# Four warm-up matmuls, two of them fp32, in place of twelve bf16 ones, in a weight-gradient kernel

## The chip, the cores and the metric

The kernel runs on one core of a Trainium2 chip. A core has a matrix engine (TensorE, "PE" in the profile, with its weight loads shown apart as "PEld"), VectorE (DVE), ScalarE (ACT), GpSimd (POOL) and SyncE (SP), each with its own instruction stream, and 16 DMA engines that they share. Engines wait for each other by semaphores. The metric is the time of one execution on the device in microseconds (us), lower is better.

## The reference

The gradient of a weight matrix: two fp32 inputs are multiplied and summed over the batch and over the rows of each batch element.

```python
batch, m, k, n = 16, 512, 1024, 768
input        # (16, 512, 1024) float32
grad_output  # (16, 512, 768)  float32
grad_weight = np.einsum('bmk,bmn->kn', input, grad_output)   # (1024, 768) float32
```

Batch and rows together make one contraction of 8192; the output has 1024 x 768 elements.

## The kernel before

The 8192 rows are cut into 64 slices of 128, since the matrix engine contracts over 128 partitions. A slice of `input` is 128 x 1024 and one of `grad_output` 128 x 768. Both output dimensions are halved (K into two halves of 512, each of four tiles of 128 columns; N into two halves of 384), so a slice needs 16 matmuls with a 128 x 128 stationary tile and a 128 x 384 moving tile, all in bf16 with fp32 sums in PSUM.

The 64 slices come in 32 loads of two. Nine loads are plain ("s" in `LOADS`): each of their slices is used in four products A, B, C and D, one for each quarter of the output. The other 23 ("P") are combined in pairs: VectorE adds and subtracts the halves of two slices, and seven products (A, D, m, n, o, p, q) do the work of eight. Their partial sums are kept in `acc` and `macc` in SBUF and carried into and out of eight PSUM banks by VectorE and ScalarE copies. Which product runs next, over how many loads, is written out by hand in the string `ORDER`; each of the four compute engines takes its instructions in program order.

The loads on the GpSimd queue convert fp32 to bf16 on the way (L113, L114, L118 and L120). The first slices are an exception, so that work can begin early: `gf` (slice 0 of `grad_output`, in two halves on SP's queue, L88 and L90) and `xf` (slices 0 and 1 of `input`, on ScalarE's queue, L89 and L91) arrive as fp32, and VectorE and ScalarE round them to bf16 piece by piece in `round_by` (L211). The first real matmuls (L337) wait for these roundings. Slice 1 of `input` is rounded just before the step that needs it.

At the very beginning stands the part that the change touches. With the four DMAs of the first slices issued, the matrix engine multiplies constant ones by constant ones twelve times (L96) into the PSUM bank `bank7`, and nothing ever reads the result. The operands are the constant tiles of the framework, written by four GpSimd memsets before the engines are let go: one column of ones, read again and again. A bf16 matmul is two instructions in the program, one that loads the stationary tile and one that streams the moving tile. The warm-up waits for nothing and, being first in the matrix engine's program, all real matmuls stand behind it.

Of the kernel before, what the change touches and what calls it, by code (L numbers as in the profile page):

```python
# [9 lines left out]
P = 128  # L10
# [25 lines left out]
    "l20 l21 l22 t20 t21 t22 t10 t11 t12 t13 l23 t23 l10 l11 l12 l13 l30 l31 l32 l33 "  # L36
).split()

WARMUP = [512] * 10 + [128] * 2
PAIRS_HELD = 14  # L40
SUMS_HELD = 9

# [4 lines left out]
def kernel(  # L47
# [6 lines left out]
    nc = tc.nc  # L54
    bf16 = mybir.dt.bfloat16
    f32 = mybir.dt.float32
# [33 lines left out]
    nc.sync.dma_start(out=gf[:, RIGHT], in_=G[0:P, RIGHT])  # L90
    nc.scalar.dma_start(out=xf[1], in_=X[P : 2 * P, :])  # L91

    ones = nc.const_aps.tensor(1.0, (P, P), bf16)
    wps = psum.tile([P, 512], f32, name="bank7")
    for cols in WARMUP:
        nc.tensor.matmul(  # L96
            wps[:, 0:cols],
            ones,
            nc.const_aps.tensor(1.0, (P, cols), bf16),
            start=True,  # L100
            stop=True,
        )
# [349 lines left out]
```

## Time and profile before

| What | Value |
|---|---|
| Time, median of 4 runs (lowest to highest) | 163.27 us (163.19 to 163.5) |
| The profiled execution's own time | 163.33 us |
| Its span, from the first to the last instruction | 161.6 us |
| PE busy | 156.6 us, 97% of the span, 950 matmuls |
| DVE / ACT / POOL busy | 140.8 / 117.9 / 34.6 us |
| Warm-up matmuls (L96) | 12 |
| Real matmuls (L337 and L392) | 938 |

The profile is one execution of the program. Times in it count from the start of the span; 1.73 us of the execution's own time lie outside it. In a timeline a row merges instructions of a kind: its start, its length, its engine and line, what it writes and reads with the shapes, how many there are, and in square brackets how long the engine had been idle before and what ended that. A matmul's end is modelled and overlaps the next one's start, so the rate of the matrix engine is read from the distance between starts, not from a matmul's length.

### The profile page before, as it was taken

How to read it: one execution, taken by the hardware profiler on the slowest of the kernel's cores; microseconds unless marked ns; L12 is line 12 of the kernel's file. 1: busy time of each engine (PE TensorE's matmuls, PEld its weight loads, DVE VectorE, ACT ScalarE, POOL GpSimd, SP SyncE). 2: the span in 40 equal slices, each digit the busy share in tenths (PEclk: the TensorE clock that was granted, in tenths of full speed). 3: DMA queues.
4: the chain of work that ended last, by engine and by line, in shares of the span. 5: the costliest groups of instructions: out<-in, count | busy, mean ns of one | idle time of the engine just before them, and what ended most of it. 6: DMA issues, size and time to landing. Idle time of an engine off the chain costs nothing.

```text
span 161.6 us, 2781 instructions
## 1 busy us (share of the span) xinstructions
PE 156.6 (97%) x950; PEld 92.7 (57%) x950; DVE 140.8 (87%) x267; ACT 117.9 (73%) x278; POOL 34.6 (21%) x69
## 2 busy tenths in 40 slices
PE   8899999999999999999999999999999999999991
PEld 2465655655556665566655566656556665556561
DVE  0545878879889999999999999999997999999982
ACT  3745348446498899978999797997795666987730
POOL 7442222212222212222222222222122100000000
PEclk9999999999999999999999999999999999999999
DMA  5999999999999999999999999999999999900695
GB/s 180 294 213 211 215 212 212 215 214 213 214 211 211 213 212 213 213 213 213 214 213 214 212 215 212 214 211 214 215 211 216 208 215 211 197 5 0 228 355 198
DMA packets 12398, 33.40 MB, mean 207 GB/s; under 512 B 1376, under 2 KB 4192, under 8 KB 12384
## 3 DMA queue, kind: packets, MB, share of 16 engines
q0 software_dynamic: 9360, 28.64, 89.6%
q1 hardware_dynamic: 2592, 3.47, 6.1%
q10 hardware_dynamic: 432, 1.11, 1.8%
q8 instruction: 7, 0.11, 0.3%
q14 instruction: 7, 0.06, 0.1%
HBM read 58.72 MB, written 3.15 MB: 383 GB/s over the span
## 4 chain that ended last, share of the span: by engine, by line
PE 84%; DMA 13%; issue 1%; DVE 0%; POOLq 0%
PE bank L337 84%; DMA xp<-in_input_dram 9%; DMA gp<-in_grad_output_dram 4%; PE bank L392 0%; DVE acc L400 0%; POOLq L436 0%
## 5 line engine op out<-in xcount | busy, mean ns | idle before, releaser
L337 PEld LDWEIGHTS <-xp 128*128 128x128 bf16 x650 | 63.3, 98 | 44.2 <-DVE xp L211 1.3
L337 PE MATMUL bank<-gp,xp 128*128 128x384 bf16 x468 | 80.8, 327 | 0.9 <-DVE xp L211 0.7
L353 ACT COPY macc<-bank 128x384 f32<-128x384 f32 x91 | 39.3, 492 | 9.8 <-PE bank L337 9.4
L357 DVE TENSOR_TENSOR acc<-bank,acc 128x384 f32<-128x384 f32 x80 | 39.8, 551 | 6.1 <-PE bank L337 5.9
L337 PEld LDWEIGHTS <-xe 128*128 128x128 bf16 x276 | 26.9, 98 | 18.0 <-DVE xe L148 0.2
L353 ACT COPY acc<-bank 128x384 f32<-128x384 f32 x57 | 24.7, 484 | 13.8 <-PE bank L337 13.8
L296 ACT COPY bank<-macc 128x384 f32<-128x384 f32 x73 | 33.0, 493 | 1.6 <-DVE acc L357 0.9
L337 PE MATMUL bank<-ge,xp 128*128 128x384 bf16 x182 | 33.6, 326 | 0.0
L337 PE MATMUL bank<-gp,xe 128*128 128x384 bf16 x184 | 32.4, 327 | 0.0
L296 ACT COPY bank<-acc 128x384 f32<-128x384 f32 x47 | 21.5, 492 | 9.1 <-DVE acc L357 7.4
L114 POOL DMA_DIRECT2D xp<-in_input_dram x30 | 15.9, 530 | 52.9 <-DMA xp<-in_input_dram 28.5
L113 POOL DMA_DIRECT2D gp<-in_grad_output_dram x30 | 15.9, 532 | 37.5 <-PE bank L337 13.9
L357 DVE TENSOR_TENSOR macc<-bank,macc 128x384 f32<-128x384 f32 x35 | 18.0, 551 | 2.0 <-PE bank L337 2.0
L138 DVE TENSOR_TENSOR ge<-gp 128x1152 bf16<-128x1152 bf16 x23 | 17.3, 751 | 0.1
L148 DVE TENSOR_TENSOR xe<-xp 128x1024 bf16<-128x1024 bf16 x23 | 15.8, 685 | 0.8 <-DMA xp<-in_input_dram 0.7
L194 DVE TENSOR_TENSOR acc<-acc,macc 128x768 f32<-128x768 f32 (+1 forms) x20 | 16.1, 874 | 0.0
L337 PE MATMUL bank<-ge,xe 128*128 128x384 bf16 x92 | 15.9, 327 | 0.0
L157 DVE TENSOR_TENSOR xp<-xp 128x1024 bf16<-128x1024 bf16 x23 | 15.8, 685 | 0.0
L143 DVE TENSOR_TENSOR gp<-gp 128x768 bf16<-128x768 bf16 x23 | 12.8, 554 | 0.5
L152 DVE TENSOR_TENSOR xe<-xp 128x512 bf16<-128x512 bf16 x23 | 9.6, 418 | 0.0
L355 DVE COPY acc<-bank 128x384 f32<-128x384 f32 x6 | 3.2, 555 | 3.1 <-PE bank L337 3.0
L96 PE MATMUL bank<-const-bfloat16-1.0 128*128 128x512 bf16 (+1 forms) x12 | 4.0, 510 | 0.8 <-PEq L436 0.8
(18 smaller groups left out, 15.6 us busy)
## 6 DMA issues: line engine op xcount, KB each, us to landing
xp<-in_input_dram POOLq DMA_DIRECT2D x30, 512.0 KB, 16.8
gp<-in_grad_output_dram POOLq DMA_DIRECT2D x30, 384.0 KB, 16.8
out_dram<-acc SPq DMA_DIRECT2D x15, 192.0 KB, 2.4
xf<-in_input_dram ACTq DMA_DIRECT2D x2, 512.0 KB, 4.9
gp<-in_grad_output_dram POOLq DMA_DIRECT2D x3, 192.0 KB, 6.4
xp<-in_input_dram POOLq DMA_DIRECT2D x2, 256.0 KB, 7.7
gf<-in_grad_output_dram SPq DMA_DIRECT2D x2, 192.0 KB, 4.2
out_dram<-acc SPq DMA_DIRECT2D x1, 128.0 KB, 1.8
```

The source lines that it names most:

```text
L113: nc.gpsimd.dma_start(out=gp, in_=G[rows, :].rearrange("(p m) n -> p m n", m=2))
L114: nc.gpsimd.dma_start(out=xp, in_=X[rows, :].rearrange("(p m) k -> p m k", m=2))
L138: nc.vector.tensor_add(out=ge.rearrange("p a n -> p (a n)"), in0=g[:, 0 : 3 * NH], in1=g[:, NH : 4 * NH])
L143: nc.vector.tensor_sub(out=g[:, 0::3, :], in0=g[:, 0::3, :], in1=g[:, 2:0:-1, :])
L148: nc.vector.tensor_add(out=xe[:, 0:2, :].rearrange("p a k -> p (a k)"), in0=xp[:, 0, :], in1=xp[:, 1, :])
L152: nc.vector.tensor_add(out=extra[i][0][:, 2, :], in0=xp[:, 0, 0:KH], in1=xp[:, 1, KH:K])
L157: nc.vector.tensor_sub(out=x[:, 1:3, :], in0=x[:, 1:3, :], in1=x[:, 0::3, :])
L194: op(out=dst, in0=dst, in1=src)
L296: nc.scalar.copy(out=bank, in_=sum_of(p, q))
L337: nc.tensor.matmul(bank, stat, mov, start=opening and j == 0 and not carried, stop=close and j == len(items_now) - 1, skip_group_check=car ...
L353: nc.scalar.copy(out=dst, in_=bank)
L357: nc.vector.tensor_add(out=dst, in0=bank, in1=dst)
```

## The change

The list `WARMUP` no longer gives twelve widths but four pairs of a type and a width, and the loop takes both operands of a matmul, stationary and moving, from the constant ones of that type. The first and the last matmul stay as they were (bf16, 512 columns); the two in the middle are fp32, 512 columns. The other eight, six of 512 columns and two of 128, are gone. An fp32 matmul is one instruction in the program, which brings its own stationary tile with it.

```diff
-WARMUP = [512] * 10 + [128] * 2
+WARMUP = [("b", 512), ("f", 512), ("f", 512), ("b", 512)]
...
-    ones = nc.const_aps.tensor(1.0, (P, P), bf16)
+
     wps = psum.tile([P, 512], f32, name="bank7")
-    for cols in WARMUP:
+    for dt, cols in WARMUP:
+        dtype = f32 if dt == "f" else bf16
         nc.tensor.matmul(
             wps[:, 0:cols],
-            ones,
-            nc.const_aps.tensor(1.0, (P, cols), bf16),
+            nc.const_aps.tensor(1.0, (P, P), dtype),
+            nc.const_aps.tensor(1.0, (P, cols), dtype),
             start=True,
             stop=True,
         )
```

The programs of the other four engines and the real part of the matrix engine's program, its waits among them, are the same instruction by instruction. The two memsets of the constants that are now read stand in both kernels.

## The prediction

> **What bounds the kernel now.** I read the chain that ended last first, because it says which part of the span can move the end at all.
>
> ```profile
> 11 pieces in order of time: start us, us, what
> ...
> 1.23 6.15 DMA gp<-in_grad_output_dram
> 7.38 0.28 issue
> 7.66 14.14 DMA xp<-in_input_dram
> 21.80 0.04 issue
> 21.84 135.47 PE bank L337 x830
> ```
>
> Up to 21.84 us the end hangs on the input transfers, and from there on the matrix engine runs without a gap: 135.47 us / 830 = 0.163 us per matmul of 384 columns. A delay of the matrix engine before 21.84 therefore reaches the end only as far as it exceeds what the engine waits there anyway. Those waits are few; the timeline of the start has all three.
>
> ```profile
> 0.78 4.01 PE L96 MATMUL bank<-const-bfloat16-1.0 128*128 128x512 bf16 x12 [0.78 <-PEq L436]
> 5.17 2.15 PE L337 MATMUL bank<-gp,xp 128*128 128x384 bf16 x12 [0.39 <-DVE xp L211]
> 7.05 0.49 DVE L211 CAST xp<-xf 128x256 bf16<-128x256 f32 x2 [0.68 <-DMA xf<-in_input_dram]
> 7.60 6.68 PE L337 MATMUL bank<-gp,xp 128*128 128x384 bf16 x40 [0.28 <-DVE xp L211]
> 21.84 0.34 PE L337 MATMUL bank<-gp,xp 128*128 128x384 bf16 x1 [0.28 <-DMA xp<-in_input_dram]
> ```
>
> The reader is to see: warm-up from 0.78 to 4.79; a first block of 12 real matmuls at 5.17, released by a rounding; a second block at 7.60, released by the rounding of a transfer that landed at 7.05; and one more wait, for a transfer, at 21.84. The idle times count from a matmul's modelled end, which lies 0.327 - 0.163 = 0.16 us after the next one could start (0.327 is the length of one). So the second and third wait are really 0.28 + 0.16 = 0.44 us each. These are two cushions: the first block may be 0.44 us late for nothing, and what is left over meets another 0.44 at 21.84.
>
> The speed of the array at the start is read from the weight loads, one in front of each warm-up matmul:
>
> ```profile
> 2.44 0.15 PEld L96 LDWEIGHTS <-const-bfloat16-1.0 128*128 128x128 bf16 x1 [0.27 <-issue]
> 2.86 0.15 PEld L96 LDWEIGHTS <-const-bfloat16-1.0 128*128 128x128 bf16 x1 [0.28 <-issue]
> 3.29 0.15 PEld L96 LDWEIGHTS <-const-bfloat16-1.0 128*128 128x128 bf16 x1 [0.27 <-issue]
> 3.72 0.15 PEld L96 LDWEIGHTS <-const-bfloat16-1.0 128*128 128x128 bf16 x1 [0.28 <-issue]
> 4.07 0.54 PEld L96 LDWEIGHTS <-const-bfloat16-1.0 128*128 128x128 bf16 x3 [0.20 <-issue]
> ```
>
> The distance is 0.427 us for 512 columns, then 0.35, and the next matmul starts (4.06 and 4.28 in narrower windows) are 0.22 apart. So the rate doubles inside the matmul that starts at 3.71: with x us at the slow rate, x/0.427 + (0.35 - x)/0.213 = 1, x = 0.27, the change lies at 3.98. That is 3.20 us after the first matmul. The row PEclk shows full clock from the first slice on, so it doesn't show this halving. The first real block is already fast (12 matmuls in 2.15 us).
>
> **What the Trainium skill says.** "TensorE: Matmul & The Clock Gate", Part 1: the array starts at half clock and is released by about 3.4 us of sustained activity, watched in windows of 3.41 us. The trace agrees: 3.20 us. The same page, Part 4: transposes don't count as busy in the same way, so not every use of the array does; the trace has none, and no fp32 either. Its section on weight-path modes: fp32 has no fast weight load. "FP8 and Floating Point Precision", TensorE Precision Notes: a true fp32 product is four passes through the array.
>
> **The change, part by part.**
>
> Removed: eight bf16 matmuls and ten weight loads of bf16 (twelve before, two after). They are before 4.79 us and nothing reads their result. The program is 18 instructions shorter; I cost that at nothing, since warm-up matmuls were paced by the array, not by issue. Without that cover it would still end in the wait for 5.17.
>
> Added: two fp32 matmuls. The trace has no row for one. Four passes of 512 columns at the slow rate are 4 x 0.427 = 1.71 us each. The warm-up is then 2 x 0.427 + 2 x 1.71 = 4.27 us at the slow rate against 10 x 0.427 + 2 x 0.107 = 4.48 before. If the rate never changes within it, it ends at 0.78 + 4.27 = 5.05, before the data at 5.17. Upper bound: every pass has its own weight load that isn't hidden, at the 0.15 us of the rows above: 8 x 0.15 = 1.2 more, end at 6.27. Lower bound: two passes each, end at 3.34. I take four passes with the loads hidden for the length, so the length alone costs nothing.
>
> Moved: the moment at which the rate doubles. This is the item with a price, and it can't be read from the trace. Bounds: from below 3.98 as before (no gain: with the data at 5.17 there is nothing to win by an earlier release), from above two windows later, 3.98 + 2 x 3.41 = 10.80. What I choose: the fp32 stream does not release the clock. In the trace the release came from a stream without a gap; an fp32 matmul brings four sets of weights in one instruction, and nothing shows that these loads slip under the passes as the bf16 ones do (PE starts 0.427 apart, loads inside). With 0.58 us per pass the array streams for 0.427/0.58 = 74% of the time. Then the real matmuls must do it: released 3.20 us after 5.17, at 8.37.
>
> The sum for that: from 5.17 to 8.37 the real matmuls run at the slow rate, 0.427 x 384/512 = 0.320 us each, so 10 of the 12 are done, and the last two take 0.163 each: the first block ends at 8.70 in place of 7.16 (7.32 less the 0.16). Its data are there (VectorE's last rounding for the first block ends at 6.37, slice 1's first pieces are rounded by 7.6). The second block starts at 8.70, not 7.60: 1.10 us late, the first cushion spent. It has the transfers that it had, and at 21.84 it finds the second cushion: 1.10 - 0.44 = 0.66 us late from there to the end, since no later wait takes anything back. Profiled execution: 161.6 + 0.66 = 162.26 of span, with 1.73 outside it 163.99; it stands 0.06 above the median of the runs, so 163.93, taken as 163.9.
>
> What is queued behind: all real matmuls, and the copies out of PSUM that wait for them; VectorE and ScalarE idle in this stretch for PE in any case. POOL's loads up to 22 us wait for transfers only, so the transfers keep their times. No wait is added, no queue is passed.
>
> **The rivals.**
>
> Covered after all (same). fp32 passes count like bf16 ones. Release at 3.98; 3.20 us of the 4.27 are done by then, the rest takes 1.07/2 = 0.53, the end is at 4.51, before 5.17. Time: 163.3. For it: warm-up had 0.39 us to spare, and the cushions make it deaf: a release at T costs (T - 5.17)/2 of the first block, so up to T = 5.17 + 2 x 0.88 = 6.93 nothing is lost, and up to 7.6 less than can be measured. Against it: a release that fails in one window comes later than that. This one ends on the other side; it decides if the release falls before 7.6.
>
> Late release, or a long warm-up (slower still). If release only comes at window ends, at 10.80: (10.80 - 5.17)/0.320 = 17.6 matmuls are done by then, which the kernel before reaches at 7.60 + 5.6 x 0.163 = 8.51; late by 2.29, less 0.44 is 1.85: 165.1. Or the loads are exposed and the clock is not released: the real block starts at 6.27, released at 9.47, ends at 9.80, late by 2.20, less 0.44 is 1.76: 165.0. For it: the windows are not tied to the first real matmul. Against it: cold real matmuls stream without a gap and should fill the next window that they can.
>
> A faster one. The two cushions are bound by transfers that landed at 7.05 and 21.80. If these landed earlier, because the program fetch of PE is shorter and leaves the DMA engines alone, up to 0.44 us at 21.84 could be won: 162.8. Against it: the instruction queues hold 7 packets each and 0.3% and 0.1% of the engines' time, and 18 instructions fewer of some 1,900 move that by nothing.
>
> **How the numbers follow.** No release by fp32, 0.36: 163.9, its own range 163.5 to 164.6. Covered, 0.33: 163.3. Late or long, 0.24: 165.1, up to 166. Faster, 0.07. About 0.2% (0.33 us) is what a measurement of this kernel can tell from no change. So slower 0.60, same 0.33, faster 0.07. The range 163.0 to 165.6 leaves out most of the faster case and the upper part of the late one, some 0.14.
>
> **What would show it.** In the timeline after: the fp32 rows at L97, their length (1.71 us each at the slow rate), and the end of warm-up. Right: the first real matmuls start 0.32 apart, the rate doubles near 8.4, the second block starts near 8.7, the wait for a transfer near 21.84 is gone. Covered: the first twelve start 0.163 apart and 7.60 and 21.84 stand. Wrong altogether: an end that moves while 21.84 stands, or real matmuls that begin after 6.3.

## The result, and the profile after

The changed kernel takes 163.11 us (median of 43 executions, 162.89 to 163.57) against 163.30 us (62 executions, 163.05 to 163.75): ratio 0.9988, 95% interval 0.9983 to 0.9992. That is 0.19 us faster. It is less than the 0.2% that the forecast called measurable, but the interval excludes no change. The forecast was 163.9 and slower. The clock did not cost what the forecast charged for it, and the kernel gained in a place that the forecast had only as its least likely case.

The timeline of the start of the changed kernel (start, length, engine, line, what), which answers to the one shown of before:

```profile
0.77 0.59 PE L97 MATMUL bank<-const-bfloat16-1.0 128*128 128x512 bf16 x1 [0.77 <-PEq L437]
...
1.15 3.62 PE L97 MATMUL bank<-const-float32-1.0 128*128 128x512 f32 x4
...
2.00 0.34 PEld L97 LDWEIGHTS bank<-const-float32-1.0 128*128 128x128 f32 x1 [0.52 <-issue]
...
2.86 0.34 PEld L97 LDWEIGHTS bank<-const-float32-1.0 128*128 128x128 f32 x1 [0.52 <-issue]
...
3.71 0.15 PEld L97 LDWEIGHTS <-const-bfloat16-1.0 128*128 128x128 bf16 x1 [0.52 <-issue]
...
4.56 0.64 PE L97 MATMUL bank<-const-bfloat16-1.0 128*128 128x512 bf16 x1
...
5.18 9.01 PE L338 MATMUL bank<-gp,xp 128*128 128x384 bf16 x51
...
7.12 0.49 DVE L212 CAST xp<-xf 128x256 bf16<-128x256 f32 x2 [0.58 <-DMA xf<-in_input_dram]
```

The two fp32 matmuls appear as four rows, with one weight load each and 0.85 us from start to start (1.15 to 4.56 is four times 0.853). That is two passes of 0.427 us per row, so four per matmul, as the forecast took it, and the 0.34 us loads are hidden under the passes. In this execution the warm-up never left the half clock: the trace's record of the full clock begins at 5.87 us (3.98 in the profile before), which is called the release below. The real matmuls begin at 5.18 all the same. The first two start 0.29 and 0.32 us before the next, the rest about 0.16 apart, and the second block starts at 7.68, right behind its rounding.

The chain that ended last, of the changed kernel:

```profile
23 pieces in order of time: start us, us, what
...
30.09 17.15 DMA xp<-in_input_dram
...
47.86 17.50 DMA xp<-in_input_dram
65.36 0.05 issue
65.41 91.93 PE bank L338 x564
```

In the profile before, the chain left the transfers at 21.84 us. Here nothing waits at 21.84; in this execution the matrix engine instead waits at 65.41 (0.39 us from start to start beyond the usual 0.16) for a later transfer. So the two profiles have the same span, 161.6 us, though the medians differ; this one execution took 163.41 us by its own time, 0.30 above its median. One profile on each side could not settle it. The forecast had listed the missing wait at 21.84 as a sign of its own case, the late release; as the experiments show, it is missing for another reason.

### The profile page after: what moved, and what is told of

The parts are those of the page before. It is cut to its first block, busy times and chain, and to the rows that moved or that the text cites. A ratio compares the mean times of both kernels' runs of the same rounds, so it can differ in the third digit from the quotient of the medians.

```text
span 161.6 us, 2769 instructions
## 1 busy us (share of the span) xinstructions
PE 157.3 (97%) x944; PEld 92.7 (57%) x944; DVE 141.2 (87%) x267; ACT 117.9 (73%) x278; POOL 34.7 (21%) x69
## 4 chain that ended last, share of the span: by engine, by line
PE 57%; DMA 38%; POOL 1%; issue 1%; DVE 0%; POOLq 0%
PE bank L338 57%; DMA xp<-in_input_dram 38%; POOL gp L119 1%; PE bank L393 0%; DVE acc L401 0%; POOL xp L121 0%; POOLq L115 0%; POOLq L437 0%; POOLq L114 0%
## 5 line engine op out<-in xcount | busy, mean ns | idle before, releaser
L297 ACT COPY bank<-acc 128x384 f32<-128x384 f32 x47 | 21.5, 492 | 8.6 <-DVE acc L358 7.0
L212 DVE CAST gp<-gf 128x192 bf16<-128x192 f32 (+1 forms) x2 | 0.7, 344 | 4.3 <-DMA gf<-in_grad_output_dram 4.3
```

The source lines that it names most:

```text
L297: nc.scalar.copy(out=bank, in_=sum_of(p, q))
```

## The experiments

All of them change only the list `WARMUP`, whose products nothing reads; every kernel computes the whole output. Ratios are against the kernel before, run beside it.

**Is the gain real, and is it the length or the number of instructions?** Four kernels on one chip.

The changed kernel again, with no edit:

> The changed kernel once more, unchanged, beside the kernel before. Theory 1 (the difference of about 0.19 us is real and belongs to the change): ratio 0.9983 to 0.9992 again, some 163.1 us against 163.3. Rival (it is chance between groups of executions, since the span of both profiles is 161.6 us): a ratio whose interval takes in 1.000. In the trace, whatever the time: the fp32 rows start 0.85 us apart while the clock is halved, and the rate doubles at a moment that differs from execution to execution (3.0 to 6.3 us after the start of the span) and has no price below about 6.9 us.

Measured: 163.08 against 163.37 us, ratio 0.9981 (0.9975 to 0.9988).

```diff
-WARMUP = [512] * 10 + [128] * 2
+WARMUP = [512] * 10
```

> The kernel before without the two last warm-up matmuls of 128 columns: ten bf16 matmuls of 512, 4.27 us at the half clock like the changed kernel's, 4.48 before. Theory 1a (the gain is the shorter warm-up: where the clock is released late, 0.78 + 4.48 = 5.26 us lies behind the data at 5.17, 0.78 + 4.27 = 5.05 doesn't): as fast as the changed kernel, ratio near 0.9988. Theory 1b (the gain is fewer instructions or the fp32 type): ratio near 1.000, at most 0.1 us gained.

Measured: 163.50 us, 1.0009 (1.0001 to 1.0017). The shorter warm-up alone wins nothing; if anything it is a little slower.

```diff
-WARMUP = [("b", 512), ("f", 512), ("f", 512), ("b", 512)]
+WARMUP = [("f", 512)] * 2 + [("b", 102)] * 10
```

> The two fp32 matmuls first, then ten bf16 matmuls of 102 columns: the same 4.27 us at the half clock and fp32 as in the changed kernel, but 22 warm-up instructions in place of 6 (24 in the kernel before). If the number of instructions makes the gain: ratio near 1.000. If the length or the fp32 type makes it: ratio near 0.9988.

Measured: 163.42 us, 1.0002 (0.9992 to 1.0011). With fp32 and the same length, but 22 instructions, the gain is gone.

The kernel before against itself:

> The kernel before against itself. Measures what the comparison finds where there is no difference: a ratio of 1.000 with an interval of some 0.0005 to either side. If it lies 0.0010 off, the difference of the changed kernel says nothing. In the trace the moment at which the rate doubles should differ from the 3.98 us of the first profile of this kernel.

Measured: 163.40 us, 1.0004 (0.9994 to 1.0013). So the gain is real, and up to here it goes with the number of instructions. The chains of the changed kernel again and of the copy of the kernel before show where:

```profile
7.83 149.26 PE bank L338 x914
```

```profile
7.70 13.96 PE bank L337 x84
21.65 0.02 issue
21.67 135.48 PE bank L337 x830
```

The changed kernel runs through from the second block to the end; the copy waits near 21.5. That wait is for a transfer, and the trace's packet and landing records tell what holds it. Each of these transfers has 16 landings in the trace, taken here as one part for each of the 16 DMA engines. Instructions are fetched by DMA as well: queue q8 of the page carries seven packets of 16 KB, about 21 us apart for most of the span, each taking some 0.9 us. The records don't name the engine that they serve. I take it for the matrix engine, because only its instructions differ between these kernels and these packets move with their number, while the other instruction queue, q14, has its first 8 KB packet within the span at 33.19 us before and at 32.86 after. The first q8 packet of the span starts close to the end of the transfer in question. From the records of six traces (us; the transfer whose first fifteen parts land near 20.5):

```
                         fetch starts   15th part lands   16th part lands
kernel before                19.77          20.41             21.80
copy of it                   19.54          20.50             21.62
ten bf16                     19.69          20.50             21.72
22 instructions              20.04          20.51             20.62
changed kernel               20.93          20.51             20.52
changed kernel again         21.02          20.41             20.63
```

In the first three rows one part of 16 is over a microsecond late. The reading is that one DMA engine is busy with the fetch; the packet records don't say which engine, so that the late part is that engine's is inferred. The timing bears it out: in the seven traces of this document whose fetch starts between 18.13 and 20.00 us the last part lands 0.75 to 1.39 us after the fifteenth, in the six from 20.04 on at most 0.22. The matrix engine needs the part 13.80 us after the start of the second block (21.40 in the kernel before: 21.84 less the wait of 0.44), at 21.4 to 21.7 us in these traces. A fetch that begins after that part has gone out does no harm there. The delay is not gone: in the changed kernel it falls on the last part of the next transfer (23.13, the fifteenth at 22.36), for which nothing waits. The 22-instruction kernel had a harmless fetch in the one execution traced, only 0.27 us from the harmful one of the kernel before; that execution took 163.18 us, 0.24 below the median, which shows no gain, so its other executions need not be alike.

**Is it the time of the fetch, or do fewer instructions simply help?** More instructions must pull the fetch forward, fewer push it back.

```diff
-WARMUP = [("b", 512), ("f", 512), ("f", 512), ("b", 512)]
+WARMUP = [("f", 512)] + [("b", 102)] * 25
```

> One fp32 matmul and 25 bf16 matmuls of 102 columns: 51 warm-up instructions (24 in the kernel before, 6 in the changed one), warm-up ends near 4.7 us, so in time. Theory (the gain comes from where the matrix engine's own instruction fetch, a 16 KB packet that starts at 19.5 to 19.8 us before and at 20.9 to 21.0 after, falls among the input transfers: at 19.8 it holds up the last sixteenth of a transfer, which lands at 21.6 to 21.8 in place of 20.6, and the matrix engine waits for it): 27 instructions more pull the fetch forward by some 1.9 us to about 17.8. It then holds up an earlier transfer, and the engine is behind by less when the one at 20.5 is due: gain, ratio near 0.9985. Rival (the fewer instructions the better): no gain, ratio 1.000 or above. What the theory leaves open: if the engine is still 1.2 us behind at 20.5, no gain either; the trace tells.

Measured: 163.05 against 163.41 us, 0.9976 (0.9967 to 0.9986): the gain of the change, with over twice the instructions of before. The fetch starts at 19.12, not 17.8, and the sixteenth part lands at 21.46, just in time. Its chain has no transfer in it after 6.5 us:

```profile
1.16 5.29 DMA gf<-in_grad_output_dram
6.46 0.03 issue
6.48 0.37 DVE gp L212
6.85 0.04 issue
6.89 150.12 PE bank L338 x918
```

```diff
-WARMUP = [("b", 512), ("f", 512), ("f", 512), ("b", 512)]
+WARMUP = [("f", 512), ("f", 512), ("f", 256)]
```

> Only fp32, 512, 512 and 256 columns: 3 instructions, the same 4.27 us at the half clock. Theory of the fetch: it starts near 21.2 us, ratio like the changed kernel's, 0.998 to 0.999. On the clock: if fp32 counts as activity, the rate doubles between 3.0 and 6.3 us as in the others; if only the bf16 matmuls at both ends had done it, the rate doubles over 2 us after the first real matmul, at 7.3 us or later, and the ratio is above 1.002.

Measured: 163.13 us, 0.9984 (0.9977 to 0.9991); fetch at 21.20, sixteenth part at 20.41. The clock was released at 6.87, a little after the 6.3 that I had named as the latest.

```diff
-WARMUP = [("b", 512), ("f", 512), ("f", 512), ("b", 512)]
+WARMUP = [("f", 512)] * 2 + [("b", 205)] * 5
```

> Two fp32 matmuls and five bf16 ones of 205 columns: 12 instructions, the same 4.27 us. Theory of the fetch: it starts near 20.5 us, after the share of its DMA engine has gone out (the fetch at 20.04 in the run with 22 instructions held nothing up), so ratio like the changed kernel's, 0.998 to 0.999. If the gain grows with every instruction left out: two thirds of it, ratio near 0.9988 to 0.999. If the gain needs the two long bf16 matmuls at the ends: ratio 1.000.

Measured: 163.34 us, 0.9996 (0.9989 to 1.0003), a miss: no gain. The fetch came at 20.00 us, not 20.5, and that is the worst place seen: the sixteenth part lands at 22.03. The timeline and the chain of this run:

```profile
6.95 14.78 PE L338 MATMUL bank<-gp,xp 128*128 128x384 bf16 x88 [0.30 <-DVE gp L212]
22.07 1.15 PE L338 MATMUL bank<-gp,xp 128*128 128x384 bf16 x6 [0.35 <-DMA xp<-in_input_dram]
```

```profile
7.88 14.15 DMA xp<-in_input_dram
22.03 0.05 issue
22.07 135.47 PE bank L338 x830
```

So the gain is not in proportion to the instructions left out: 12 do no better than 24, while 6, 3 and 51 all gain. In the executions traced, the fetch at 20.00 delays the part and the one at 20.04 (22 instructions) doesn't.

**Does fp32 matter at all?** Two warm-ups of bf16 alone with many instructions:

```diff
-WARMUP = [512] * 10 + [128] * 2
+WARMUP = [512] * 6 + [102] * 20
```

> No fp32 at all: six bf16 matmuls of 512 columns and twenty of 102, 52 instructions, some 4.3 us at the half clock. Theory of the fetch: like the run with 51 instructions (fetch near 19.0 us, the held-up sixteenth lands by about 21.4, just when the matrix engine needs it), ratio 0.9970 to 0.9988. Rival (the gain also needs fp32 in the warm-up, which the runs with 6, 3 and 51 instructions all had): ratio 0.9995 to 1.001, as for ten bf16 matmuls.

Measured: 163.10 against 163.48 us, 0.9977 (0.9967 to 0.9987); fetch at 19.22, sixteenth part at 21.39, and nothing waits from the second block on:

```profile
7.61 149.30 PE bank L337 x914
```

```diff
-WARMUP = [512] * 10 + [128] * 2
+WARMUP = [512] * 4 + [102] * 29
```

> Four bf16 matmuls of 512 columns and twenty-nine of 102, 66 instructions, some 4.2 us at the half clock. Theory of the fetch: it starts near 18.0 us, the held-up sixteenth lands near 20.0 and is no longer late; ratio 0.997 to 0.9985, at best a little under the changed kernel's. If fetching early is bad in itself: above 0.999.

Measured: 163.02 us, 0.9968 (0.9956 to 0.9979). The ratio lies just under the range expected (0.997 to 0.9985); the reason came out only in part: the fetch starts at 18.13, but the sixteenth part still lands at 21.37, not 20.0. The next transfer has a last part that is late as well (23.24, the one ahead of it 22.43), as if the engine that fetched stayed behind for some time. It is early enough all the same: by its rate from the second block (7.81 + 13.80) the matrix engine gets there at 21.61. This is the lowest ratio measured, but its interval overlaps with that of the changed kernel (0.9975 to 0.9988, on another chip), so the two are not told apart. The gain needs no fp32.

**Does fp32 release the clock, and what would a failed warm-up have cost?**

```diff
-WARMUP = [("b", 512), ("f", 512), ("f", 512), ("b", 512)]
+WARMUP = [("b", 512)] + [("f", 512)] * 6 + [("b", 512)]
```

> One bf16 matmul, six fp32 ones, one bf16: the fp32 stretch lasts some 10 us at the half clock and 5 at the full one. If fp32 counts as activity, the distance between fp32 rows falls from 0.85 to 0.43 us within the stretch, 2.7 to 6.1 us after its start, and the real matmuls begin near 8 us at the full clock. If it doesn't: all twelve fp32 rows 0.85 us apart, real matmuls from about 11.9 us, at the half clock.

Measured in one execution: 166.62 us. The weight loads of the fp32 rows show the step directly:

```profile
5.42 0.33 PEld L97 LDWEIGHTS bank<-const-float32-1.0 128*128 128x128 f32 x1 [0.52 <-issue]
6.28 0.33 PEld L97 LDWEIGHTS bank<-const-float32-1.0 128*128 128x128 f32 x1 [0.52 <-issue]
6.90 0.19 PEld L97 LDWEIGHTS bank<-const-float32-1.0 128*128 128x128 f32 x1 [0.29 <-issue]
7.33 0.19 PEld L97 LDWEIGHTS bank<-const-float32-1.0 128*128 128x128 f32 x1 [0.24 <-issue]
7.77 0.19 PEld L97 LDWEIGHTS bank<-const-float32-1.0 128*128 128x128 f32 x1 [0.24 <-issue]
```

Distances of 0.86, then 0.62, then 0.43: the rate doubles at 6.66 us by the clock record, inside a stretch of nothing but fp32 that had begun at 1.16. So fp32 matmuls do release the clock.

```diff
-WARMUP = [("b", 512), ("f", 512), ("f", 512), ("b", 512)]
+WARMUP = [("b", 512)] * 3
```

> Three bf16 matmuls of 512 columns, no fp32: 6 warm-up instructions as in the changed kernel, but the warm-up ends near 2.1 us. The price of a warm-up that fails: real matmuls start at the half clock at 5.17 and the rate doubles at 7.3 to 10.7 us. By the reckoning of the forecast (late by half of the slow time, less a cushion of 0.44 in the first block and what is left to wait near 21 us): 0.2 to 1.8 us slower than the changed kernel, some 0.8 in the mean, ratio near 1.003 against before. If the cushions take more than reckoned: near 0.999.

Measured: 164.55 against 163.41 us, 1.0076 (1.0054 to 1.0098; four executions from 164.30 to 165.22; the slowest is the one traced). Also 6 instructions, but the warm-up is over by 2.1 us. The clock is released at 10.74 in the execution traced, the second block starts at 8.99, and the last matmul starts at 159.86 in place of 158.08: 1.78 us late. The forecast's reckoning for a release at 10.74 gives, as for its late case, (10.74 - 5.17)/0.320 = 17.4 matmuls done, which the kernel before has at 7.60 + 5.4 x 0.163 = 8.48; late by 2.26, less the cushion of 0.44 is 1.82. The difference of the medians is smaller, 1.14 us: the other three executions, which have no trace, were 0.59 to 0.92 us shorter.

## Why the prediction was wrong

**What bounds the kernel: right, and it carries the explanation.** From the start of the second block to the start of the last matmul the traces show 150.48 us before and 150.04 in the changed kernel again; less the wait of 0.44 at 21.84, before also has 150.04. The same sum with the 0.51 of the 12-instruction run (150.58) gives 150.07, with the 0.18 of the copy (150.22) 150.04. So this wait is all that separates these executions behind the second block. The first profile of the changed kernel fits too: 150.43 less its wait of 0.39 at 65 is 150.04.

**The two cushions: right.** Releases at 6.66, 6.75 and 6.87 us (ten bf16, 22 instructions, three fp32) moved the second block only to 7.85, 7.90 and 7.96, and their last matmuls start at 158.01, 157.91 and 157.98, not later than before's 158.08 with a release at 3.98. The limit of 6.93 that the forecast worked out was not crossed. It holds against the kernel before only. Where the wait at 21 is gone, as in the runs with 22 instructions and three fp32, the second cushion is gone with it, and what the second block loses to a late release reaches the end: the changed kernel again, released at 3.41, starts that block at 7.83 and its last matmul at 157.87.

**The length of the warm-up: right.** Four passes, loads hidden, 4.27 us at the half clock. The trace shows two weight loads for each fp32 matmul, where the forecast reckoned with four sets.

**The moment of the release: the step that failed.** I took it that the fp32 stream does not release the clock, because its weight loads might leave gaps. The loads are hidden, so there are no gaps. In the two profiles of the changed kernel the release came at 5.87 and at 3.41 us, the latter within the fp32 rows, and not at 8.37; the long fp32 stretch shows it with fp32 alone. The 0.66 us built on the step never arose; its arithmetic held in the run with three bf16 matmuls, where the warm-up does fail. The Trainium skill's "TensorE: Matmul & The Clock Gate", Part 1, says the windows run freely and the release varies by about 0.5 us; the spread here is larger, 3.41 to 6.87 us over traces of warm-ups of nearly one length.

**The faster rival: right in kind, dismissed for the wrong reason.** It named the shorter program fetch of the matrix engine and the wait at 21.84, at most 0.44 us. I gave it 0.07 because the fetch is 0.3% of the DMA time and 18 instructions change that by nothing. The amount indeed didn't change, 7 packets of 16 KB both times. What changed was when one of them starts, 19.5 to 19.8 against 20.9 to 21.0 us, and one packet held up the one part of a transfer that the matrix engine then waited for. I costed "18 instructions fewer" at nothing and didn't ask what is triggered by the place in the program. The term was mis-sized at 0; measured, 0.19 and 0.29 us in two comparisons.

That the gain is less than 0.44 fits the traces. The five traces of kernels without it wait 0.44, 0.18 (the copy), 0.14 (ten bf16), 0 (22 instructions) and 0.51 us at 21; one execution of each doesn't show how these waits are spread over the others. And the changed kernel can lose at 65 what it gains at 21, in the same way: in its first profile the third fetch starts at 63.32, the fifteenth part of a transfer lands at 64.49 and the sixteenth only at 65.36, and the matrix engine waits for it until 65.41. In its second profile that fetch starts at 63.49, the sixteenth part lands at 64.59 and nothing waits. The kernels with 51, 52 and 66 instructions have this fetch at 58.5 to 59.9, long before, which may be why they gain more (0.36 to 0.46 us); that was not tested. Nor did any run move the fetches by other means than the warm-up.

**The range: luck.** That 163.11 lies within the stated 163.0 to 165.6 says nothing for the mechanism: the low end was there for the case of no change.

## What to carry to other kernels

By the timing in these traces, the matrix engine's own instruction fetches compete with the data for the DMA engines; where a wait for a transfer ends last, compare their times with that transfer's slowest part, not their share of the traffic. A change in the number of early instructions, whatever its purpose, moves all later fetches, so a difference of 0.1 to 0.3% after such a change should be tested with a version that has the same work and another instruction count before it is credited to the idea. For a warm-up, reckon how late the release may come without costing time before reckoning when it comes.

## What the runs showed of the hardware

- A true fp32 matmul of 512 columns: two rows of two passes each, 1.71 us at the half clock and 0.86 at the full one; each row's weight load takes 0.34 and 0.19 us and lies under the passes.
- In all thirteen traces the stretch at full clock lasted 157.01 or 153.60 us, which differ by 3.41 us and are 46 and 45 times that: release and renewed halving both fall on a grid of 3.41 us, whose phase differs from execution to execution.
- How much of a window must be busy is not sharply settled: an execution was released at 3.41 us with the array busy since 0.77 (bf16, then fp32), another was not released at 3.46 (its release at 6.87 less 3.41; fp32 only, busy since 0.77), and one was not at 7.33 (10.74 less 3.41) with bf16 since 5.18.
- A fetch of 16 KB takes some 0.9 us, and a transfer under way at that time can have one of its 16 parts land over 1 us late (1.39 us in the kernel before). In another execution, with a start 0.04 us later (20.04 in place of 20.00), the part was on time.
